# Output projection by pairs of token tiles, with the first feed-forward columns ahead of the last transposes

## The chip, the cores and the metric

The kernel runs on one core of one Trainium2 chip. The metric is the device time of one execution in microseconds (us). Before the change it is 950.52 us, the median of three runs (950.33 to 952.98). Engines are named as in the profile: PE (TensorE) does matmuls and transposes, PEld is its weight load, DVE (VectorE), ACT (ScalarE) and POOL (GpSimd) do elementwise work, and SP issues most DMAs.

## The reference, cut to what matters

One encoder block on 512 tokens and 16 learned meta tokens, width 1024, float32. Two branches (stick-breaking attention and gated linear attention) are merged by gates into `mix_in`; the change begins behind that.

```python
mix = (gate_sb * (sb @ w_sb_out) + gate_gla * (o @ w_gla_out)) @ w_o      # 528 x 1024
h = h + rmsnorm(mix, norm_mix_post)
hn = rmsnorm(h, norm_ffn_pre)
up = hn @ w_ffn_up                                                        # 528 x 2816
act = gelu(causal_dwconv(up, conv_w, conv_b))                             # 3 taps along the tokens
ffn = (act * (hn @ w_ffn_gate)) @ w_ffn_down
h = h + rmsnorm(ffn, norm_ffn_post)                                       # meta tokens dropped
```

## The kernel before, in words

Every float32 product is made of three fp32r matmuls: each operand is split into a high part (a cast on ACT) and a low part (operand minus high part), and high times high, high times low and low times high are added in PSUM. For a weight, `load_w` (lines 79 to 92) does one DMA from SP into a `raw` tile of 512 KB, one cast on ACT (`wh`, L90) and one subtraction on POOL (`wl`, L91). There are three `raw` buffers, and two `wh` and two `wl` buffers in the pool `wp`; a second pool `wx` has two more of each.

The output projection (`mix_in @ w_o`) works on four token tiles of 128 and on two column halves of 512. The right half of `w_o` (`woh`, `wol`) is loaded while the merged input is still being made (loop over `j` from L795). The left half comes in four loads `oa0` to `oa6`, each of two row blocks `k`; each load is used for all four token tiles (L909 to L919, 96 matmuls of 512 columns, "wo" in the trace), so all four left halves are finished together, in the two 1024-column PSUM buffers `wo01` and `wo23`. Those two are the only buffers of their tag (`mm`), which the feed-forward's `pt_up` uses later. The right half is done tile by tile in `second(i)` (24 matmuls each, "wob"), in PSUM buffers of tag `z` (two). The product for the two meta tokens that the convolution needs is made from the `raw` tiles by `meta_products` (L787), so a `raw` tile is held until those matmuls are done.

Behind each half `gained` (L835) takes the sum of squares on ACT and the gain on DVE; `normed` (L849) then does, for one token tile, two RMS norms, the residual and the product `y`, and transposes `y` on PE (8 transposes, "ht"), with a cast on ACT and a subtraction on DVE for each half (`split`, L136) into `h2h` and `h2l`, which hold the normed hidden state with the tokens along the columns. `mini` (L871) is the same chain for the two meta tokens, in pieces.

The feed-forward loops over 22 column tiles `m`: `pt_up` (L965, 48 matmuls of 256 or 258 columns, tokens 0 to 255 and then the others) and `ga` (L981 to L986). For `m` of 0 and 1 both are done in two token halves, so that tokens 0 to 255 (tiles 1 and 2) can be multiplied before tiles 3 and 4 are transposed.

The order on each engine is fixed before the run by a planner (`schedule_with_timeline_sim`, L1195). It goes by the program's order and lets later work pass ahead where it expects the earlier not to be ready; buffers are given out in the order in which they are taken. `tc.issue_after(x)` puts an instruction behind `x` in the queue of the same engine. Three such pins stand around the change: two transposes are set behind matmuls 8 and 16 of the last `second` (`CUT`, L928), and the casts of the first two gate tiles are set behind a step of tile 2's norm (`GA`, L944 and L979). Each engine takes its own queue strictly in that order.

Of the kernel before, what the change touches and what calls it, by code (L numbers as in the profile page):

```python
# [43 lines left out]
GA = 3  # L44
CUT = (8, 16)
# [6 lines left out]
def block_kernel(ctx: ExitStack, tc: tile.TileContext, x, meta_tokens, norm_mix_pre, w_in, w_gk_up, b_gk,  # L52
# [47 lines left out]
    def proj(w, xh, xl, segs, name, apart=False):  # L100

        wh, wl = w
        nk, m = wh.shape[1], wh.shape[2]
        (l0, l1), (_, l2) = segs
        pt = mmt(f"pt_{name}")
        segs = [(pt[:m, 512 - l1 + l0 : 512], l0, l1), (pt[:m, 512 : 512 + l2 - l1], l1, l2)]
        steps = [(k, a, b) for k in range(nk) for a, b in ((wh, xh), (wh, xl), (wl, xh))]
        for grp in ([[s] for s in segs] if apart else [segs]):
            for n, (k, a, b) in enumerate(steps):
                for dst, lo, hi in grp:  # L110
                    pe.matmul(dst, a[:, k, :], b[:, k, lo:hi], start=n == 0, stop=n == len(steps) - 1)  # L111
        return pt[:m, 512 - l1 + l0 : 512 + l2 - l1]
# [712 lines left out]
    with tc.tile_pool(name="pw", bufs=1) as pw:  # L825
# [22 lines left out]

        def normed(i):  # L849

            t, h, xi = slice((i - 1) * P, i * P), hb[:, i - 1, :], xr[:, i - 1, :]
# [7 lines left out]
            y = pw.tile([P, D], F32, tag="y", name=f"y{i}", bufs=2)  # L859
            for b in range(2):  # L860
                c = slice(b * 512, b * 512 + 512)
                dve.scalar_tensor_tensor(out=y[:, c], in0=h[:, c], scalar=r, in1=g2bc[:, c], op0=ALU.mult, op1=ALU.mult)
            for b in range(2):
# [38 lines left out]

        ones = pw.tile([P, P], F32, name="ones")
# [3 lines left out]
        pos = [mmt("wo01"), mmt("wo23")]  # L907
        d0 = [pos[i // 2][:, (i % 2) * 512 : (i % 2) * 512 + 512] for i in range(4)]
        for k in range(8):  # L909
            if k % 2 == 0:  # L910
                wh, wl = load_w(wrows(w_o, k, 2, 0, 512), 2, f"oa{k}")
                raw = last_raw[0]
            a, b = wh[:, k % 2, :], wl[:, k % 2, :]
            for i in range(4):
                t = slice(i * P + NM - T0, i * P + P + NM - T0)
                for q, (m, w) in enumerate(((mh, a), (mh, b), (ml, a))):
                    pe.matmul(d0[i], m[k][:, t], w, start=k == 0 and q == 0, stop=k == 7 and q == 2)  # L917
            if k % 2:
                meta_products(k - 1, 0, raw)  # L919

        last_mm = [None]

        def second(i):
# [3 lines left out]
            for q, (a, b) in enumerate(ops):  # L927
                after = sum(q >= c for c in CUT) if i == 4 else 0  # L928
                with tc.issue_after(last_ht[after].ins) if after else ExitStack():
                    last_mm[0] = pe.matmul(pt, a, b, start=q == 0, stop=q == len(ops) - 1)  # L930
# [32 lines left out]
    with tc.tile_pool(name="pu", bufs=2) as pu:  # L963
        for m in range(FT):
            pt = proj(load_w(cols(w_up, m * P), KT, f"up{m}", into=wx if m % 2 else None), h2h, h2l, FFNS, f"up{m}", apart=m < 2)  # L965
# [16 lines left out]
            for lo, hi in ((0, 256), (256, 512)) if m < 2 else ((0, 512),):  # L982
                for k in range(KT):
                    for q, (a, b) in enumerate(((wh, h2h), (wh, h2l), (wl, h2h))):
                        pe.matmul(pg_[:, lo:hi], a[:, k, :], b[:, k, lo:hi], start=lo == 0 and k == 0 and q == 0,  # L985
                                  stop=k == KT - 1 and q == 2, skip_group_check=True)  # L986
# [212 lines left out]
```

## Time and profile before

| what | value |
|---|---|
| median of three runs | 950.52 us |
| profiled execution | 952.2 us |
| its span in the trace | 950.5 us |
| PE busy | 924.2 us, 97% of the span |
| DVE, ACT, POOL busy | 67%, 52%, 37% |
| granted PE clock, mean | 0.992 of full |

The profiled execution is 1.7 us above the median and 1.7 us longer than its own span. A row of a timeline gives the start in us from the span's beginning, the time of the group, and in square brackets how long the engine stood idle before it and what released it. The end of a matmul is modelled and overlaps the next one, so the pace is read from start to start. The granted clock is a share of 2.4 GHz; 0.5 is 1.2 GHz.

### The profile page before, as it was taken

The page shows a single profiled execution, that of the slowest core. Times are in us where ns is not written, and L with a number is a line of the kernel's source. Part 1 is how long each engine was busy: PE and PEld are TensorE (multiplying, and loading weights), DVE is VectorE, ACT ScalarE, POOL GpSimd, SP SyncE. Part 2 cuts the span into 40 slices and gives each one's busy share as a digit, 9 for nine tenths or more (in the row PEclk, how much of TensorE's full clock was granted, in tenths as well). Part 3 has the DMA queues.
Part 4 walks back from the last instruction along what each step waited for, and adds up shares of the span by engine and source line. Part 5 has one row for each costly group of instructions (what it writes and reads, how often), then busy time and mean ns, then how long its engine had stood idle before and what let it go on. Part 6 is the DMA issues. An engine that isn't in the chain of part 4 may idle for free.

```text
span 950.5 us, 17905 instructions
## 1 busy us (share of the span) xinstructions
PE 924.2 (97%) x7229; PEld 846.2 (89%) x7229; DVE 632.4 (67%) x1080; ACT 492.2 (52%) x934; POOL 351.3 (37%) x259
## 2 busy tenths in 40 slices
PE   7999999999999998999999998999999999999996
PEld 7999999999999998999998677999999999988785
DVE  6676858677558785887847347555554445588987
ACT  5664656566467674676664244533333333355654
POOL 5433242333345444554445432444444444100100
PEclk9999999999999999999999998999999999999999
DMA  7122222212222212231214643333333333274923
GB/s 212 53 69 68 69 68 68 68 46 72 65 75 80 67 48 66 67 90 46 78 56 130 212 124 112 89 104 98 89 89 90 100 99 89 89 258 159 266 81 123
DMA packets 129876, 93.39 MB, mean 98 GB/s; under 512 B 4080, under 2 KB 114930, under 8 KB 129794
## 3 DMA queue, kind: packets, MB, share of 16 engines
q1 hardware_dynamic: 126178, 82.55, 29.1%
q10 hardware_dynamic: 2112, 6.82, 1.9%
q0 software_dynamic: 1504, 2.88, 1.8%
q8 instruction: 57, 0.93, 0.4%
q14 instruction: 25, 0.20, 0.1%
HBM read 88.05 MB, written 4.19 MB: 97 GB/s over the span
## 4 chain that ended last, share of the span: by engine, by line
PE 86%; DVE 7%; issue 2%; ACT 2%; POOL 1%; SPq 1%; DMA 1%; DVEq 0%; POOLq 0%; ACTq 0%
PE pt_up L111 13%; PE ga L985 13%; PE pt_gv L111 5%; PE pt_gr L111 5%; PE pt_mg L111 4%; PE pt_go L111 4%; PE pt_ms L111 3%; PE dA L1047 3%; PE dD L1047 3%; PE pt_gk L111 3%; PE pt_so L111 2%; PE pt_gq L111 2%; PE dB L1047 2%; PE wo L917 2%; PE pt_sv L111 2%
## 5 line engine op out<-in xcount | busy, mean ns | idle before, releaser
L91 POOL TENSOR_TENSOR wl_up<-raw_up,wh_up 128x1024 fp32r<-128x1024 f32 x22 | 52.9, 2407 | 85.1 <-ACT wh_up L90 85.1
L91 POOL TENSOR_TENSOR wl_ga<-raw_ga,wh_ga 128x1024 fp32r<-128x1024 f32 x22 | 55.6, 2530 | 71.9 <-ACT wh_ga L90 71.9
L111 PE MATMUL pt_up<-h2l,wh_up 128*128 128x256 f32 (+1 forms) x352 | 73.5, 283 | 0.0
L111 PE MATMUL pt_up<-h2h,wh_up 128*128 128x256 f32 (+1 forms) x352 | 73.4, 283 | 0.0
L111 PE MATMUL pt_up<-h2h,wl_up 128*128 128x256 f32 (+1 forms) x352 | 73.4, 282 | 0.0
L985 PE MATMUL ga<-h2l,wh_ga 128*128 128x512 f32 (+1 forms) x192 | 72.2, 376 | 0.2 <-DVE h2l L139 0.2
L985 PE MATMUL ga<-h2h,wh_ga 128*128 128x512 f32 (+1 forms) x192 | 72.0, 376 | 0.2 <-ACT h2h L138 0.2
L985 PE MATMUL ga<-h2h,wl_ga 128*128 128x512 f32 (+1 forms) x192 | 72.1, 376 | 0.0
L90 ACT CAST wh_up<-raw_up 128x1024 fp32r<-128x1024 f32 x22 | 23.1, 1050 | 79.2 <-PE pt_up L111 67.2
L111 PEld LDWEIGHTS pt_up<-h2h,wh_up 128*128 128x128 f32 x352 | 57.0, 189 | 1.8
L111 PEld LDWEIGHTS pt_up<-h2l,wh_up 128*128 128x128 f32 x352 | 55.5, 189 | 0.0
L111 PEld LDWEIGHTS pt_up<-h2h,wl_up 128*128 128x128 f32 x352 | 55.4, 189 | 0.0
L985 PEld LDWEIGHTS ga<-h2h,wl_ga 128*128 128x128 f32 x192 | 36.2, 188 | 7.0
L985 PEld LDWEIGHTS ga<-h2l,wh_ga 128*128 128x128 f32 x192 | 36.1, 188 | 6.6 <-DVE h2l L139 0.4
L985 PEld LDWEIGHTS ga<-h2h,wh_ga 128*128 128x128 f32 x192 | 36.1, 188 | 6.6 <-ACT h2h L138 0.5
L976 DVE SCALAR_TENSOR_TENSOR cy<-pt_up,cw,cy 128x511 f32<-128x511 f32 (+1 forms) x22 | 16.4, 746 | 36.8 <-ACT cy L973 36.8
L976 DVE SCALAR_TENSOR_TENSOR yp<-pt_up,cw,yp 128x511 f32<-128x511 f32 (+1 forms) x22 | 16.4, 745 | 31.2 <-ACT yp L973 31.2
L90 ACT CAST wh_ga<-raw_ga 128x1024 fp32r<-128x1024 f32 x22 | 22.9, 1047 | 26.1 <-PE ga L985 24.3
L138 ACT CAST sh_p<-As 128x512 fp32r<-128x512 f32 (+1 forms) x30 | 17.4, 584 | 29.6 <-PE dB L1047 12.9
L91 POOL TENSOR_TENSOR wl_gr<-raw_gr,wh_gr 128x1024 fp32r<-128x1024 f32 x8 | 19.1, 2387 | 36.0 <-ACT wh_gr L90 27.1
L1075 POOL DMA_DIRECT2D tv<-in_w_ffn_down_dram x6 | 7.1, 1177 | 68.2 <-DVE wl_p L139 68.2
L111 PE MATMUL pt_gr<-hnh,wh_gr 128*128 128x258 f32 (+1 forms) x128 | 28.2, 294 | 0.0
(558 smaller groups left out, 3179.4 us busy)
## 6 DMA issues: line engine op xcount, KB each, us to landing
raw_up<-in_w_ffn_up_dram SPq DMA_DIRECT2D x22, 512.0 KB, 3.8
raw_ga<-in_w_ffn_gate_dram SPq DMA_DIRECT2D x22, 512.0 KB, 3.8
raw_t<-in_w_ffn_down_dram SPq DMA_DIRECT2D x10, 512.0 KB, 7.2
raw_gv<-in_w_in_dram SPq DMA_DIRECT2D x8, 512.0 KB, 3.9
raw_gr<-in_w_in_dram SPq DMA_DIRECT2D x8, 512.0 KB, 3.8
raw_mg<-in_w_in_dram SPq DMA_DIRECT2D x8, 512.0 KB, 3.9
raw_go<-in_w_gla_out_dram SPq DMA_DIRECT2D x8, 512.0 KB, 4.2
raw_ms<-in_w_in_dram SPq DMA_DIRECT2D x8, 512.0 KB, 3.9
```

Source lines behind the costliest of these rows:

```text
L90: act.copy(hi_out, raw)
L91: lo_eng.tensor_tensor(out=lo_out, in0=raw, in1=f32(hi_out), op=ALU.subtract)
L111: pe.matmul(dst, a[:, k, :], b[:, k, lo:hi], start=n == 0, stop=n == len(steps) - 1)
L138: act.copy(hi, src)
L917: pe.matmul(d0[i], m[k][:, t], w, start=k == 0 and q == 0, stop=k == 7 and q == 2)
L976: dve.scalar_tensor_tensor(out=y[:, d:], in0=pt[:, : SEQ - d], scalar=c, in1=y[:, d:], op0=ALU.mult, op1=ALU.add)
L985: pe.matmul(pg_[:, lo:hi], a[:, k, :], b[:, k, lo:hi], start=lo == 0 and k == 0 and q == 0, stop=k == KT - 1 and q == 2, skip_group_check= ...
L1047: mm[i] = pe.matmul(dsts[i], a, b, start=first and k == 0 and j == 0, stop=last and k == NP - 1 and j == 2, skip_group_check=True)
L1075: return lambda n, q, nk: pool.dma_start(out=t[:, q : q + nk, :], in_=block(s, c, q, nk), accum_op=ALU.add)
```

## The change

The left half of the projection is done by `halves(g)` for two token tiles at a time: first tiles 1 and 2 into `wo12`, later tiles 3 and 4 into `wo34`. Each of the two passes loads all four row-block pairs, so the left half of `w_o` is fetched, cast and subtracted twice. The right halves of tiles 1 and 2 go ahead of the first pass. The norm chain of tiles 1 and 2 (`mixed`, which is `gained` twice and `normed`) stands between the passes, and behind it the weights of the first two `up` tiles, both into `wx`. The transposes are taken out of `normed` into `turned`; those of tiles 1 and 2 are pinned behind the second pass. Then come `second(3)`, `second(4)` with the pieces of `mini`, the weights of the first two gate tiles, and for tokens 0 to 255 the products of the first two `up` and the first two gate tiles; the transposes of tile 3 are pinned behind the first of these gate products, those of tile 4 behind the second. The loop over `m` then does only the rest of these four products. The pins `CUT` and `GA` are gone.

```diff
-        pos = [mmt("wo01"), mmt("wo23")]
-        d0 = [pos[i // 2][:, (i % 2) * 512 : (i % 2) * 512 + 512] for i in range(4)]
-        for k in range(8):
-            if k % 2 == 0:
-                wh, wl = load_w(wrows(w_o, k, 2, 0, 512), 2, f"oa{k}")
-                raw = last_raw[0]
-            a, b = wh[:, k % 2, :], wl[:, k % 2, :]
-            for i in range(4):
...
+        pos = [mmt("wo12"), mmt("wo34")]
+        def halves(g):
+            for k in range(8):
+                if k % 2 == 0:
+                    wh, wl = load_w(wrows(w_o, k, 2, 0, 512), 2, f"oa{g}{k}")
+                    raw = last_raw[0]
+                a, b = wh[:, k % 2, :], wl[:, k % 2, :]
+                for i in range(2):
+                    t = slice((2 * g + i) * P + NM - T0, (2 * g + i + 1) * P + NM - T0)
+                    for q, (m, w) in enumerate(((mh, a), (mh, b), (ml, a))):
+                        last_mm[0] = pe.matmul(pos[g][:, i * 512 : i * 512 + 512], m[k][:, t], w, start=k == 0 and q == 0, stop=k == 7 and q == 2)
+                if k % 2 and g == 0:
+                    meta_products(k - 1, 0, raw)
+
+        def mixed(i, pt):
+            gained(i, pos[(i - 1) // 2][:, (i - 1) % 2 * 512 : (i - 1) % 2 * 512 + 512], 0)
+            gained(i, pt, 1)
+            normed(i)
...
-        gained(1, second(1), 1)
-        for i in (1, 2, 3, 4):
-            gained(i, d0[i - 1], 0)
+        early = [second(1), second(2)]
+        halves(0)
+        for i in (1, 2):
+            mixed(i, early[i - 1])
+        ups = [load_w(cols(w_up, m * P), KT, f"up{m}", into=wx) for m in range(2)]
+        halves(1)
+        with tc.issue_after(last_mm[0].ins):
+            turned(1)
+            turned(2)
         m = mini()
-        for i in (2, 3, 4):
+        for i in (3, 4):
             pt = second(i)
-            if i > 2:
-                with tc.issue_after(last_mm[0].ins):
-                    next(m)
-            gained(i, pt, 1)
-            normed(i - 1)
-            if i == GA:
-                late = last_exp[0]
+            with tc.issue_after(last_mm[0].ins):
+                next(m)
+            mixed(i, pt)
+        gas = [load_w(cols(w_gate, m * P), KT, f"ga{m}") for m in range(2)]
         next(m)
-        normed(4)
+
+        begun = [proj(ups[m], h2h, h2l, FFNS, f"up{m}", apart=True, only=(0,)) for m in range(2)]
+        pgs_ = []
+        for m in range(2):
+            pgs_.append(pst(f"ga{m}", "z"))
+            gate_half(pgs_[m], gas[m], 0, 256)
+            with tc.issue_after(last_ga[0].ins):
+                turned(3 + m)
...
-            pt = proj(load_w(cols(w_up, m * P), KT, f"up{m}", into=wx if m % 2 else None), h2h, h2l, FFNS, f"up{m}", apart=m < 2)
+            if m < 2:
+                pt = proj(ups[m], h2h, h2l, FFNS, f"up{m}", apart=True, only=(1,), pt=begun[m])
+            else:
+                pt = proj(load_w(cols(w_up, m * P), KT, f"up{m}", into=wx if m % 2 else None), h2h, h2l, FFNS, f"up{m}")
...
-            with tc.issue_after(late.ins) if m < 2 else ExitStack():
-                wh, wl = load_w(cols(w_gate, m * P), KT, f"ga{m}", into=wx if m % 2 else None)
-            pg_ = pst(f"ga{m}", "z")
...
+            if m < 2:
+                pg_ = pgs_[m]
+                gate_half(pg_, gas[m], 256, 512)
+            else:
+                pg_ = pst(f"ga{m}", "z")
+                gate_half(pg_, load_w(cols(w_gate, m * P), KT, f"ga{m}", into=wx if m % 2 else None), 0, 512)
```

## Rows read from the trace of the kernel before

**Rows 1.** the page: busy shares, and the chain that ended last by engine.

```profile
PE 924.2 (97%) x7229; PEld 846.2 (89%) x7229; DVE 632.4 (67%) x1080; ACT 492.2 (52%) x934; POOL 351.3 (37%) x259
...
PE 86%; DVE 7%; issue 2%; ACT 2%; POOL 1%; SPq 1%; DMA 1%; DVEq 0%; POOLq 0%; ACTq 0%
```

**Rows 2.** busy time of PE, PEld, DVE, ACT, POOL; clock; DMA share; GB/s.

```profile
526.00:544.00 18.00, 18.00 (x93) 12.46 (x91) 6.12 (x6) 2.56 (x4) 4.26 (x3) 1.00 0.66 235
...
572.00:582.00 10.00, 6.28 (x25) 5.22 (x26) 7.50 (x17) 4.70 (x12) 5.27 (x2) 0.66 0.49 156
```

**Rows 3.** PE in order of time: start, us, line, operation, tiles.

```profile
566.62 0.40 PE L930 MATMUL wob<-wol,mh 128*128 128x512 f32 x1
567.81 1.38 PE L867 MATMUL ht<-ident,y 128*128 128x128 f32 x8 [0.79 <-DVE y L862]
568.94 0.48 PE L930 MATMUL wob<-woh,ml 128*128 128x512 f32 x1
...
570.64 0.40 PE L930 MATMUL wob<-woh,mh 128*128 128x512 f32 x1
570.97 0.71 PE L880 MATMUL mini<-sel,mc 128*32 128x2 f32 x64
574.04 1.09 PE L867 MATMUL ht<-ident,y 128*128 128x128 f32 x4 [2.36 <-DVE y L862]
...
577.55 0.78 PE L930 MATMUL wob<-wol,mh 128*128 128x512 f32 x1
...
580.96 0.28 PE L111 MATMUL pt_up<-h2h,wh_up 128*128 128x256 f32 x1
```

**Rows 4.** the same view, at full pace, and around the last tile's transposes.

```profile
559.32 0.39 PE L930 MATMUL wob<-woh,mh 128*128 128x512 f32 x1
...
564.68 0.40 PE L930 MATMUL wob<-woh,ml 128*128 128x512 f32 x1
...
584.37 0.28 PE L985 MATMUL ga<-h2h,wl_ga 128*128 128x256 f32 x1
...
586.87 0.28 PE L985 MATMUL ga<-h2h,wl_ga 128*128 128x256 f32 x1
...
589.03 0.60 PE L867 MATMUL ht<-ident,y 128*128 128x128 f32 x4
589.39 0.37 PE L111 MATMUL pt_up<-h2h,wh_up 128*128 128x256 f32 x1
...
593.67 1.07 PE L867 MATMUL ht<-ident,y 128*128 128x128 f32 x8
...
595.71 0.39 PE L985 MATMUL ga<-h2l,wh_ga 128*128 128x256 f32 x1 [0.23 <-DVE h2l L139]
```

**Rows 5.** the same view, where the first four row blocks of L917 end.

```profile
543.39 0.40 PE L917 MATMUL wo<-wh_oa,ml 128*128 128x512 f32 x1
...
544.26 0.50 PE L930 MATMUL wob<-woh,mh 128*128 128x512 f32 x1
```

**Rows 6.** DMA queue of SP, in order of time.

```profile
519.40 19.08 SPq L85 DMA_DIRECT2D raw_oa<-in_w_o_dram  x4
...
549.10 0.37 SPq L85 DMA_DIRECT2D raw_up<-in_w_ffn_up_dram  x1
```

**Rows 7.** ACT in order of time, the third cast of L917's weights.

```profile
543.18 1.05 ACT L90 CAST wh_oa<-raw_oa 128x1024 fp32r<-128x1024 f32 x1 [11.32 <-DMA raw_oa<-in_w_o_dram]
```

**Rows 8.** POOL in order of time: subtractions of L917's weights and of the gate's.

```profile
544.31 4.76 POOL L91 TENSOR_TENSOR wl_oa<-raw_oa,wh_oa 128x1024 fp32r<-128x1024 f32 x2 [12.84 <-ACT wh_oa L90]
...
573.62 5.27 POOL L91 TENSOR_TENSOR wl_ga<-raw_ga,wh_ga 128x1024 fp32r<-128x1024 f32 x2 [14.77 <-ACT wh_ga L90]
```

**Rows 9.** the page: DMA issues, KB each, median us to landing.

```profile
raw_up<-in_w_ffn_up_dram SPq DMA_DIRECT2D x22, 512.0 KB, 3.8
```

**Rows 10.** one tile, y: duration ns min/median/max, first and last start.

```profile
L862 DVE SCALAR_TENSOR_TENSOR y<-hb,a_ffn,g2bc x8: 744/748/2846, 567.0 to 593.2; 128x512 f32<-128x512 f32 x8
```

**Rows 11.** DVE in order of time, the last tile's y.

```profile
592.49 1.42 DVE L862 SCALAR_TENSOR_TENSOR y<-hb,a_ffn,g2bc 128x512 f32<-128x512 f32 x2
```

More of the change, by code (lines that the diff above doesn't have):

```diff
@@ L43 @@
 EASY = 4
-GA = 3
-CUT = (8, 16)
 EARLY = 3
@@ L98, in wrows, with proj @@
         return w[k0 * P : (k0 + nk) * P, c0:c1].rearrange("(k p) m -> p k m", p=P)
-    def proj(w, xh, xl, segs, name, apart=False):
+    last_pr = [None]
+    def proj(w, xh, xl, segs, name, apart=False, only=None, pt=None):
         wh, wl = w
@@ L104, in proj @@
         (l0, l1), (_, l2) = segs
-        pt = mmt(f"pt_{name}")
+        begins = only and pt is None
+        pt = mmt(f"pt_{name}") if pt is None else pt
         segs = [(pt[:m, 512 - l1 + l0 : 512], l0, l1), (pt[:m, 512 : 512 + l2 - l1], l1, l2)]
         steps = [(k, a, b) for k in range(nk) for a, b in ((wh, xh), (wh, xl), (wl, xh))]
+        segs = [segs[i] for i in only] if only else segs
         for grp in ([[s] for s in segs] if apart else [segs]):
@@ L110, in proj @@
                 for dst, lo, hi in grp:
-                    pe.matmul(dst, a[:, k, :], b[:, k, lo:hi], start=n == 0, stop=n == len(steps) - 1)
-        return pt[:m, 512 - l1 + l0 : 512 + l2 - l1]
+                    last_pr[0] = pe.matmul(dst, a[:, k, :], b[:, k, lo:hi], start=n == 0, stop=n == len(steps) - 1)
+        return pt if begins else pt[:m, 512 - l1 + l0 : 512 + l2 - l1]
     last_exp = [None]
@@ L901, in mini, with gate_half @@
             yield
+        last_ga = [None]
+        def gate_half(pt, w, lo, hi):
+            wh, wl = w
+            for k in range(KT):
+                for q, (a, b) in enumerate(((wh, h2h), (wh, h2l), (wl, h2h))):
+                    last_ga[0] = pe.matmul(pt[:, lo:hi], a[:, k, :], b[:, k, lo:hi], start=lo == 0 and k == 0 and q == 0,
+                                           stop=k == KT - 1 and q == 2, skip_group_check=True)
         ones = pw.tile([P, P], F32, name="ones")
         pool.memset(ones, 1.0)
-        pos = [mmt("wo01"), mmt("wo23")]
-        d0 = [pos[i // 2][:, (i % 2) * 512 : (i % 2) * 512 + 512] for i in range(4)]
-        for k in range(8):
-            if k % 2 == 0:
-                wh, wl = load_w(wrows(w_o, k, 2, 0, 512), 2, f"oa{k}")
-                raw = last_raw[0]
-            a, b = wh[:, k % 2, :], wl[:, k % 2, :]
-            for i in range(4):
[L915 to L919, printed above, removed]
-        last_mm = [None]
+        pos = [mmt("wo12"), mmt("wo34")]
+        last_mm = [None]
+        def halves(g):
[14 more added lines that the diff above has]
+            normed(i)
         def second(i):
@@ L927, in second @@
             for q, (a, b) in enumerate(ops):
-                after = sum(q >= c for c in CUT) if i == 4 else 0
-                with tc.issue_after(last_ht[after].ins) if after else ExitStack():
-                    last_mm[0] = pe.matmul(pt, a, b, start=q == 0, stop=q == len(ops) - 1)
-            return pt
-        gained(1, second(1), 1)
-        for i in (1, 2, 3, 4):
-            gained(i, d0[i - 1], 0)
+                last_mm[0] = pe.matmul(pt, a, b, start=q == 0, stop=q == len(ops) - 1)
+            return pt
+        early = [second(1), second(2)]
[7 more added lines that the diff above has]
+            turned(2)
         m = mini()
-        for i in (2, 3, 4):
+        for i in (3, 4):
             pt = second(i)
-            if i > 2:
-                with tc.issue_after(last_mm[0].ins):
-                    next(m)
-            gained(i, pt, 1)
-            normed(i - 1)
-            if i == GA:
-                late = last_exp[0]
-        next(m)
-        normed(4)
+            with tc.issue_after(last_mm[0].ins):
+                next(m)
+            mixed(i, pt)
+        gas = [load_w(cols(w_gate, m * P), KT, f"ga{m}") for m in range(2)]
+        next(m)
+        begun = [proj(ups[m], h2h, h2l, FFNS, f"up{m}", apart=True, only=(0,)) for m in range(2)]
[5 more added lines that the diff above has]
+                turned(3 + m)
         for i in range(4):
```

12 lines of the change are left out of this document (5 added, 7 removed).

## The prediction, made before the changed kernel had run

> **What bounds the kernel now.** Three views are read, from the coarse to the fine. The page comes first: PE is busy for 97% of the span and makes 86% of the chain that ended last [rows 1]. With the same matmuls before and after, time can only come from stretches in which PE stands still or runs slowly, so the next view is the busy time by stretch. In 526 to 544, where the left half of the projection runs, PE is busy for all 18.00 us at a clock of 1.00. In 572 to 582 it is busy for 6.28 of 10.00 us, and the mean clock is 0.66, so part of what is left runs at 1.2 GHz [rows 2]. The third view, PE in order of time, says what the holes are [rows 3]. I count them from start to start against the full pace: 23 steps of 512 columns take 564.68 - 559.32 = 5.36 us, 0.233 each; 21 steps of 256 columns take 2.50 us, 0.119 each; four transposes between matmuls take 0.36 us, so eight take 0.72 [rows 4].
>
> The holes [rows 3]:
> - From the end of the matmul at 566.62 (566.62 + 0.23 = 566.85) to the next projection matmul at 568.94 are 2.09 us with 0.72 us of transposes in them: 1.37 lost, waiting for `y` of tile 1.
> - From 570.64 + 0.23 = 570.87 to 577.55 are 6.68 us with 0.71 of `mini` and 0.72 of transposes: 5.25 lost, waiting for `y` of tile 2.
> - From 577.55 to 580.96 are 3.41 us for eight matmuls of 0.233 (1.86): 1.55 lost. PE had just stood idle, and the clock stands at its lower level.
>
> Together 8.2 us: the most that this change can take out here. The wait behind the last tile's transposes (2.04 us from 593.67 to 595.71, of which 0.72 are transposes, so 1.3 [rows 4]) stays, since tile 4 is still the last.
>
> **What the change leaves equal.** L917 has 8 x 4 x 3 = 96 matmuls before and 2 x 8 x 2 x 3 = 96 after. The 96 of `second`, the transposes, and the products of the first two `up` and gate tiles (already in two halves of the tokens before) are the same in number and shape. PE's own work changes by nothing.
>
> **What goes.** The norms of tiles 1 and 2 can start when the first pass ends, with 48 matmuls of the second pass (48 x 0.233 = 11.2 us) ahead of their transposes. Tile 3's transposes have three half products, 3 x 24 x 0.119 = 8.6 us, ahead of them and tile 4's have four, 11.4 us; before, they were set between the last eight projection matmuls and the first feed-forward ones. If the norms are done in time, all three holes go: -8.2 us.
>
> **What the second fetch costs.** Four more loads are issued on SP. Before, each load fed 24 matmuls, 24 x 0.233 = 5.6 us; now each feeds 12, 2.8 us. For each, ACT casts for 1.05 us [rows 7] and POOL subtracts for 2.4 (4.76 for two [rows 8]), 3.5 us one behind the other; with two buffers for the split weights, the third load waits until PE has done with the first. So loads are now slower than PE wherever PE has nothing else. SP's queue matters as well: it waited in the midst of its four issues of these loads, which stretch over 19.08 us, for the three raw buffers, and the buffer of the fourth came free for a later weight at 549.10, when POOL ended [rows 6, 8]. In the new order the first `up` weights stand ahead of the second pass on SP, ACT and POOL. Nothing else queued on these engines there is on the path; what waits behind are the second pass's own weights.
>
> POOL's queue from 544.31 [rows 8] is then eight subtractions: two for the first pass, two for `up`, four for the second pass. 8 x 2.4 = 19.2 brings it to 563.5. A raw buffer freed at 549.10 and a landing of 3.8 [rows 9] and a cast of 1.05 give 554.0, about when POOL comes to it (544.31 + 4 x 2.4 = 553.9), so the transfers hide behind POOL. The third load of the pass waits for PE to free a buffer: its predecessor's twelve matmuls, a cast and the hand-over cost POOL some 1.9. So the last subtraction ends near 565.4, and eleven matmuls behind it end the second pass near 568.0.
>
> PE meanwhile: the 48 matmuls of row blocks 0 to 3 end at 543.6 before, and ten matmuls of `second` still come behind them from 544.26 on [rows 5]. Now only 24 are there, and the ten come first: 543.6 - 24 x 0.233 + 10 x 0.233 = 540.3. The next weights are cast at 543.18 whatever PE does, since their transfer sets it [rows 7]. From 540.3 to 568.0 are 27.7 us; PE has 72 matmuls of L917 (16.8) and the meta products (1.1) for it. A hole of 9.8 us is left, and what can fill it are the 48 matmuls of tiles 3 and 4's right half, 11.2 us. They need the PSUM buffers of tiles 1 and 2, which come free after a square and a gain; ACT stands idle for 11.32 us just there [rows 7]. The planner does such filling today: ten `second` matmuls stand where the third load comes late [rows 5]. The bounds are 0 (filled) and 9.8 (not). I take it as filled, but with POOL late: DVE operations with two operands in SBUF and POOL's subtractions hold each other up. One `y` took 2846 ns against a median of 748 [rows 10], during two subtractions that took 5.27 together where two took 4.76 [rows 8]. Some five of the norms' eight such operations fall on POOL's chain and push it by 5 x 0.6 = 3.0: the pass ends at 571.0, PE's own work at 540.3 + 17.9 + 11.2 = 569.4, and 1.6 us are lost.
>
> The Trainium skill, "SBUF — State Buffer", section "Who interferes with whom", says that a DVE instruction with two inputs in SBUF and a GpSimd instruction that reads SBUF exclude each other for a whole instruction. The long `y` agrees. By that rule alone each of the eight operations can wait a whole subtraction, which is the slower rival below and not my sum.
>
> **What is late next.** With the filler used up, nothing covers the split of tiles 1 and 2 behind their transposes. The bounds are 0 (some `second` left over) and 2.6 (twice the wait of one tile [rows 4]); I take that one wait, 1.3. Then tile 4: before, 592.49 + 1.42 - 580.96 = 12.9 us lay between the end of its projection [rows 3] and its `y` [rows 11]. In the new order tile 3's norm starts at the same moment and four splits and the gate's subtractions lie beside. The cover is 1.4 (transposes) + 1.3 + 0.7 (`mini`) + 11.4 + 0.4 = 15.2. Four more DVE splits at some 0.7, an estimate from the 1.3 above, make 15.7, so 0.5 is lost; the bounds are 0 and 4.2, where two `y` meet the gate's subtractions (2.1 each [rows 10]). The pins that kept these subtractions away are gone.
>
> **Sum.** -8.2 + 1.6 + 1.3 + 0.5 = -4.8 us. The profiled execution took 952.2, which gives 947.4; it lies 1.7 above the median of the runs shown, so against 950.5 the forecast is 945.7. By the bounds of the last terms it lies between 943.0 and 948.0.
>
> **Rivals.**
> - Everything hides: 950.5 - 8.2 = 942.3. For it speaks that the filler (11.2) is larger than the hole (9.8); against it, that POOL has no slack.
> - The gain is given back in the two passes, because the filler is only partly put into the holes: some half of 9.8 stays, 4.9 in place of 1.6, with the split and tile 4's lateness as above: -8.2 + 4.9 + 1.8 = -1.5, 949.0; its range is 947.7 to 953.3. For it speaks that PE takes its queue in order, so a filler set behind a late weight helps nothing; against it, that the planner's filling before fits the transfers [rows 5].
> - Slower: the transposes of tiles 1 and 2 wait for `y` at the head of PE's queue. They are pinned behind the second pass, and DVE must do eight two-operand operations beside POOL's closed chain of eight subtractions. At 2.85 us each [rows 10] they take 22.8 us; from some 554.5, when the first squares and gains are done, `y` of tile 2 comes at 577.3 where my sum has PE ready at 571.0. That is 6.3 lost, and with the idle time the lower clock as in the third hole, 1.5. With 1.6, 1.3 and 2.6 for tile 4, which starts later on DVE, the sum is -8.2 + 13.3 = +5.1: 955.6. It decides from the point where more than about six of the eight wait out a subtraction. For it speaks the one long `y`; against it, that POOL's chain ends near 568, after which nothing holds DVE.
>
> **How the numbers follow.** Chances: forecast 0.42, everything hides 0.15, given back 0.25, slower 0.18. About 0.3%, 2.9 us, is what a measurement of this kernel can tell from no change. Faster by more than that (below 947.6): the first two, 0.57. Within it (947.6 to 953.4): nearly all of the third and a little of the others, 0.25. Slower: 0.18. The range that leaves out 2 in 10 is 941.9 to 953.3: it takes in everything hidden and the third case, and leaves out the slower one. The forecast's own range is 943.0 to 948.0.
>
> **What would show it.** The three holes gone: PE without idle time ahead of the transposes of tiles 1 and 2, and at clock 1.00 up to the feed-forward. Matmuls of tiles 3 and 4's right half among those of L917. POOL closed with eight subtractions and PE's second pass ending near 568 to 571. The prediction is wrong if L917 stands still for more than 2 us in its passes, if the first transposes wait for `y` for more than 2 us, or if the hole comes back at tile 4's transposes.

## The result, and the profile after

The changed kernel takes 957.56 us (median of six runs, 955.25 to 959.0) against 951.55 for the kernel before on the same chip: a ratio of 1.006, interval 1.0042 to 1.0078. It is slower by 0.6%; the forecast was 945.7, and the range ended at 953.3.

The page shows no change that would explain it: PE's busy time is 1.4 us longer than in [rows 1], and its share of the span and of the chain are the same. The page of after, busy shares and the chain by engine:

```profile
PE 925.6 (97%) x7229; PEld 847.4 (89%) x7229; DVE 640.5 (67%) x1080; ACT 496.6 (52%) x938; POOL 360.7 (38%) x263
...
PE 86%; DVE 6%; issue 2%; ACT 2%; DMA 2%; POOL 1%; DVEq 0%; ACTq 0%; POOLq 0%; SPq 0%
```

So the place must be found by stretch. From the first right-half matmul to the first matmul of the third `up` tile, the same work lies in both kernels: 103.6 us before (503.44 to 607.03), 111.1 after (502.06 to 613.12), 7.5 more. The profiled execution of after took 957.73, 5.5 more than before's: its earlier part was 1.4 shorter, the part behind 0.6. The stretches of [rows 2] in after, with those behind each of them (columns as there):

```profile
526.00:544.00 18.00, 14.91 (x81) 9.06 (x79) 4.86 (x6) 2.61 (x3) 4.14 (x4) 1.00 0.72 257
544.00:560.00 16.00, 13.26 (x48) 9.68 (x49) 6.00 (x8) 8.22 (x14) 12.95 (x6) 0.79 0.58 175
...
572.00:582.00 10.00, 8.20 (x41) 6.33 (x39) 6.05 (x8) 4.45 (x10) 6.84 (x3) 1.00 0.40 122
582.00:596.00 14.00, 13.03 (x145) 12.79 (x146) 12.02 (x38) 7.50 (x26) 0.30 (x1) 0.76 0.33 115
```

526 to 544, where PE was full before, now has 3.1 us without work, and the clock falls in the stretch behind. 572 to 582 is better than before (8.20 in place of 6.28, clock 1.00), and 582 to 596 has the low clock that used to stand there. PE in after, in order of time:

```profile
539.18 0.61 PE L793 MATMUL meta<-raw_oa,m 128*2 128x256 f32 x8
541.68 0.61 PE L793 MATMUL meta<-raw_oa,m 128*2 128x256 f32 x8 [1.89 <-DMA raw_oa<-in_w_o_dram]
542.83 0.50 PE L936 MATMUL wo<-wh_oa,mh 128*128 128x512 f32 x1 [0.54 <-ACT wh_oa L88]
544.21 0.70 PE L793 MATMUL meta<-raw_oa,m 128*2 128x256 f32 x8 [0.88 <-DMA raw_oa<-in_w_o_dram]
545.26 0.79 PE L936 MATMUL wo<-wl_oa,mh 128*128 128x512 f32 x1 [0.34 <-POOL wl_oa L89]
545.85 0.63 PE L936 MATMUL wo<-wh_oa,ml 128*128 128x512 f32 x1
...
548.25 0.40 PE L936 MATMUL wo<-wh_oa,ml 128*128 128x512 f32 x1
...
552.77 0.50 PE L936 MATMUL wo<-wh_oa,mh 128*128 128x512 f32 x1 [0.65 <-ACT wh_oa L88]
554.81 0.79 PE L950 MATMUL wob<-woh,mh 128*128 128x512 f32 x1 [1.53 <-DVE hb L842]
...
578.04 1.04 PE L875 MATMUL ht<-ident,y 128*128 128x128 f32 x8
...
581.13 0.66 PE L875 MATMUL ht<-ident,y 128*128 128x128 f32 x4 [1.59 <-DVE h2l L141]
582.97 1.12 PE L875 MATMUL ht<-ident,y 128*128 128x128 f32 x4 [1.18 <-DVE v_mix L125]
...
588.99 0.29 PE L917 MATMUL ga<-h2h,wl_ga 128*128 128x256 f32 x1
```

Counted from start to start against the pace of [rows 4], as before, and a group of eight meta products at the 0.55 us that it takes where nothing waits:
- In the first pass, from 539.18 to 545.26, 4.2 us are lost waiting for the left half's weights; behind that the matmuls run at half pace until 548.25 (seven steps: one of 0.59, five of 0.43, a last one of 0.27), 1.4 lost. At 552.77 and 554.81 another 2.6 are lost, and 1.7 of low clock up to 558.33. Together 9.9: 6.8 of waiting and 3.1 of low clock.
- The second pass runs at full pace and ends at 578.04. The transposes of tile 1 follow at once. Those of tile 2 lose 3.2 us of waiting at 581.13 and 582.97, and until 588.99 PE runs at half pace: 2.7. Together 5.9.
- The three holes of [rows 3], 8.2, are gone. The last transposes lose 1.6 where the same count gives 1.1 before.

-8.2 + 9.9 + 5.9 + 0.5 = 8.1 against the 7.5 measured in the stretch; 0.6 is not assigned.

Why does nothing fill the first hole? ACT and DVE in after, around the end of the first pass:

```profile
541.74 1.04 ACT L88 CAST wh_oa<-raw_oa 128x1024 fp32r<-128x1024 f32 x1 [11.13 <-DMA raw_oa<-in_w_o_dram]
...
552.63 0.59 ACT L841 ACTIVATE wj<-wo 128x512 f32<-128x512 f32 x1
...
553.34 0.60 ACT L841 ACTIVATE wj<-wob 128x512 f32<-128x512 f32 x1
```

```profile
553.34 0.69 DVE L842 TENSOR_TENSOR hb<-wo,g1bc 128x512 f32<-128x512 f32 x1 [22.01 <-DMA raw_oa<-in_w_o_dram]
554.06 0.69 DVE L842 TENSOR_TENSOR hb<-wob,g1bc 128x512 f32<-128x512 f32 x1
```

ACT stands idle for 11.13 us, as it did before [rows 7], but the right half's square (`wj<-wob`) does not use them: it comes at 553.34, behind the left half's (`wj<-wo`) at 552.63, and its gain at 554.06. The matmul at 554.81, the first of tile 3's right half, is released by that gain: until then both buffers of tag `z` hold the right halves of tiles 1 and 2. The squares of both halves write into one scratch buffer (`junk`). `mixed` takes it for the left half first, and buffers are given out in the order in which the program takes them.

### The profile page after: what moved, and what is told of

Read it like the earlier page. It is cut to its first block, busy times and chain, and to the rows that moved or that the text cites. A ratio compares the mean times of both kernels' runs of the same rounds, so it can differ in the third digit from the quotient of the medians.

```text
span 956.0 us, 17918 instructions
## 1 busy us (share of the span) xinstructions
PE 925.6 (97%) x7229; PEld 847.4 (89%) x7229; DVE 640.5 (67%) x1080; ACT 496.6 (52%) x938; POOL 360.7 (38%) x263
## 4 chain that ended last, share of the span: by engine, by line
PE 86%; DVE 6%; issue 2%; ACT 2%; DMA 2%; POOL 1%; DVEq 0%; ACTq 0%; POOLq 0%; SPq 0%
PE pt_up L113 13%; PE ga L917 13%; PE pt_gv L113 5%; PE pt_gr L113 4%; PE pt_mg L113 4%; PE pt_ms L113 4%; PE pt_go L113 4%; PE dA L1078 3%; PE dD L1078 3%; PE wob L950 3%; PE pt_gk L113 3%; PE pt_so L113 2%; PE pt_gq L113 2%; PE dB L1078 2%; PE pt_sv L113 2%
## 5 line engine op out<-in xcount | busy, mean ns | idle before, releaser
L917 PE MATMUL ga<-h2l,wh_ga 128*128 128x512 f32 (+1 forms) x192 | 72.3, 377 | 0.0
L917 PE MATMUL ga<-h2h,wh_ga 128*128 128x512 f32 (+1 forms) x192 | 72.3, 377 | 0.0
L917 PE MATMUL ga<-h2h,wl_ga 128*128 128x512 f32 (+1 forms) x192 | 72.2, 377 | 0.0
L917 PEld LDWEIGHTS ga<-h2h,wl_ga 128*128 128x128 f32 x192 | 36.4, 190 | 7.0
L917 PEld LDWEIGHTS ga<-h2l,wh_ga 128*128 128x128 f32 x192 | 36.4, 190 | 6.2
L917 PEld LDWEIGHTS ga<-h2h,wh_ga 128*128 128x128 f32 x192 | 36.4, 190 | 6.0
L89 POOL TENSOR_TENSOR wl_oa<-raw_oa,wh_oa 128x1024 fp32r<-128x1024 f32 x8 | 19.3, 2415 | 24.8 <-ACT wh_oa L88 24.6
```

What stands on the lines that cost most here:

```text
L89: lo_eng.tensor_tensor(out=lo_out, in0=raw, in1=f32(hi_out), op=ALU.subtract)
L917: last_ga[0] = pe.matmul(pt[:, lo:hi], a[:, k, :], b[:, k, lo:hi], start=lo == 0 and k == 0 and q == 0, stop=k == KT - 1 and q == 2, skip_ ...
```

## The experiments

Each kernel was timed against the kernel before on the same chip. "Stretch" is the time from the first right-half matmul to the third `up` tile, as above, in its profiled execution (103.6 before, 111.1 after).

| kernel | median | before | ratio, interval | stretch |
|---|---|---|---|---|
| e2_columns_only | 952.2 | 950.63 | 1.0012, 1.0002 to 1.0021 | 103.8 |
| e3_pairs_only | 967.53 | 950.63 | 1.0172, 1.0157 to 1.0187 | 119.3 |
| e1_release | 953.81 | 950.63 | 1.0032, 1.0018 to 1.0047 | 106.7 |
| e4_keep | 956.12 | 950.63 | 1.0057, 1.0038 to 1.0075 | 107.6 |
| f_after | 954.5 | 951.67 | 1.0028, 1.0016 to 1.0041 | 106.7 |
| f_before | 951.71 | 951.67 | 0.9999, 0.9989 to 1.0009 | 103.4 |
| e6_release_pin | 952.57 | 951.67 | 1.0006, 0.9996 to 1.0016 | 104.2 |
| f_e7 | 951.84 | 951.67 | 1.0003, 0.9993 to 1.0013 | 103.2 |
| f_e9 | 952.27 | 951.8 | 1.0008, 0.9999 to 1.0017 | 104.8 |
| f_e10 | 956.72 | 951.8 | 1.0057, 1.0043 to 1.0072 | 108.6 |
| f_e11 | 951.79 | 950.7 | 1.0004, 0.9995 to 1.0013 | 103.1 |
| f_e12 | 952.69 | 950.7 | 1.001, 1.0001 to 1.0019 | 104.2 |

### Each part alone

The expectations speak of three theories. A: the buffers that the filling matmuls need are not free in time. B: the second fetch is too slow. C: the order of the transposes is the fault. A and B are taken up in the next part.

The second part alone: one pass over four tiles as before, the first two `up` and gate tiles ahead. In the code of all runs "..." stands for lines left out.

```diff
-        def halves(g):
+        def halves():
...
-                for i in range(2):
...
+                for i in range(4):
...
-        early = [second(1), second(2)]
-        halves(0)
-        for i in (1, 2):
-            mixed(i, early[i - 1])
...
-        halves(1)
...
+        halves()
+        for i in (1, 2):
+            gained(i, second(i), 1)
+        for i in (1, 2):
+            gained(i, pos[0][:, (i - 1) * 512 : i * 512], 0)
+            normed(i)
```

> The second part of the change alone: the left half is done in one pass for four tiles with one fetch, as before; the transposes of tiles 1 and 2 are pinned behind the right half of tile 4, and the first columns of two up and two gate tiles stand ahead of the transposes of tiles 3 and 4, as in the change. Theories A and B both put the loss into the two passes, so this part keeps most of the 8.2 us of the holes, less some 3 to 4 for the split of tiles 1 and 2 that nothing covers: 946 to 948. Theory C (the order of the transposes is the fault: in the changed kernel 3.6 us of waiting and 2.4 us of low clock around the transposes of tile 2): 951 to 955.

The first part alone: two passes, and the `up` and gate loads and products back in the loop over `m`.

```diff
-        ups = [load_w(cols(w_up, m * P), KT, f"up{m}", into=wx) for m in range(2)]
...
+            turned(i)
...
-        begun = [proj(ups[m], h2h, h2l, FFNS, f"up{m}", apart=True, only=(0,)) for m in range(2)]
...
-            gate_half(pgs_[m], gas[m], 0, 256)
...
+            pt = proj(load_w(cols(w_up, m * P), KT, f"up{m}", into=wx if m % 2 else None), h2h, h2l, FFNS, f"up{m}", apart=m < 2)
```

> The first part alone: two passes with the second fetch and the transposes of tiles 1 and 2 behind the second pass, as in the change; the first up and gate tiles and their loads stand in the loop again and the transposes of tiles 3 and 4 directly behind their norms. Theories A and B: the holes in the passes stay as in the changed kernel, 956 to 960. Theory C: the loss goes with the moved columns, 950 to 953.

The second part alone makes 1.0012, 0.2 us more in the stretch: with the norms where they were it gains nothing. Its 952.2 lies in theory C's range and not in that of A and B. The wait of [rows 3] for tile 2's `y` is still there. PE of e2_columns_only:

```profile
572.63 0.40 PE L896 MATMUL msmix<-msqmix,ones 128*128 128x16 f32 x2 [1.99 <-DVE h2l L141]
575.24 1.89 PE L875 MATMUL ht<-ident,y 128*128 128x128 f32 x8 [2.21 <-DVE y L866]
```

The first part alone costs 15.7 us of stretch, more than any theory allowed for, and the 950 to 953 that theory C gave for it is out. It has the first hole of after in its passes (of the second only 0.63 us is left), and behind them two longer ones: one ahead of tile 2's transposes, and one for the split of the last tiles, which the products of the columns cover in after. PE of e3_pairs_only:

```profile
584.31 1.97 PE L875 MATMUL ht<-ident,y 128*128 128x128 f32 x8 [6.38 <-DVE h2l L141]
...
614.57 0.70 PE L113 MATMUL pt_up<-h2h,wh_up 128*128 128x258 f32 x2 [4.91 <-ACT h2h L140]
```

So the loss sits in the first part, and the two parts don't add: 15.7 + 0.2 alone, 7.5 together.

### What empties the passes

Two theories: the right halves' buffers are not free because their squares wait for the scratch buffer's turn, or the loads of the second fetch are too slow for PE whatever stands beside them. The first is tested twice: by the program's order, and by the place that the square writes to.

```diff
+        for i in (1, 2):                            # e1_release
+            gained(i, early[i - 1], 1)
         halves(0)
         for i in (1, 2):
-            mixed(i, early[i - 1])
+            gained(i, pos[0][:, (i - 1) * 512 : i * 512], 0)
+            normed(i)
```

> The changed kernel with one edit: square and gain of the right halves of tiles 1 and 2 stand ahead of the first pass, so that their two PSUM buffers come free before it. Theory A (release): the trace of the changed kernel has PE waiting 4.2 us at 539.7 to 545.3 and 2.6 us at 552.0 to 554.8, with 3.0 us of low clock behind them, because the matmuls that should fill these holes could not get a buffer before the gain at 554.06; with the edit they fill them, 9.8 us go, some 2 come back where POOL's subtractions end later than the filler lasts: 949 to 951. Theory B (second fetch): the second pass ends when POOL's and ACT's queue of loads ends, whatever PE does in between: 956 to 958.

```diff
-            junk = pw.tile([P, 512], F32, tag="junk", name=f"wj{i}_{hf}")       # f_after, f_before
-            act.activation(junk, pt, AF.Square, accum_out=sq[:, i, hf : hf + 1])
+            act.activation(hb[:, i - 1, c], pt, AF.Square, accum_out=sq[:, i, hf : hf + 1])
```

> The changed kernel with its order as it is and one edit: the squares of the two halves are written over the slice of hb that the gain then fills, in place of the one scratch buffer (junk) that all squares share. Theory A, made sharper: the right halves of tiles 1 and 2 kept their PSUM buffers because the one scratch buffer is given out in program order, left half first; with the edit the holes of 9.8 us in the passes close without any reordering, as in the run with the moved gains, and tile 2's squares no longer stand behind tile 1's norm: 950 to 953. Rival (the gain's place in the program decides, not the scratch buffer): 956 to 958.

> The kernel before with only the scratch buffer taken out of the four halves' squares. Theory A and D: there the right halves' buffers are not what PE waits for, and the order of PE hardly changes, but tile 2's squares can go ahead of tile 1's norm, so the waits for y (6.6 us) shrink by up to 2: 948.5 to 950.5. Rival: no change, 950 to 951.

The second theory is tested by fetching less: the second pass begins with the row blocks 4 to 7 that are still held.

```diff
-            for k in range(8):                                                  # e4_keep
+            ks = (4, 5, 6, 7, 0, 1, 2, 3) if g else range(8)
+            for k in ks:
                 if k % 2 == 0:
-                    wh, wl = load_w(wrows(w_o, k, 2, 0, 512), 2, f"oa{g}{k}")
+                    if not (g and k >= 4):
+                        held[k] = load_w(wrows(w_o, k, 2, 0, 512), 2, f"oa{g}{k}")
+                    wh, wl = held[k]
```

> The changed kernel with two loads fewer: the second pass begins with row blocks 4 to 7, whose split weights are still in their buffers, and fetches only row blocks 0 to 3 again. Theory B (second fetch): two casts (2.1 us), two subtractions (4.8 us) and two transfers of 512 KB go, and the second pass starts without waiting for a load: 951 to 953. Theory A (release): the wait of 4.2 us for the third load of the first pass and the low clock behind it (1.4) stay, the 2.6 us between the passes and the 1.7 behind them go: 953 to 954.

Either way of freeing the squares fills the passes, though both times (953.81 and 954.5) lie above what theory A gave for them. The stretches 526 to 544 and 544 to 560 in f_after, where only the place of the squares is changed:

```profile
526.00:544.00 18.00, 18.00 (x90) 12.13 (x89) 6.04 (x8) 3.60 (x7) 4.21 (x4) 1.00 0.74 255
544.00:560.00 16.00, 16.00 (x81) 11.90 (x80) 5.79 (x9) 8.44 (x15) 13.31 (x6) 1.00 0.62 175
```

3.09 and 2.74 us of idle time and the low clock are gone, with the four extra loads still there. What is left in the passes is one wait for a late subtraction. PE of e1_release and then of f_after:

```profile
565.21 0.50 PE L936 MATMUL wo<-wl_oa,mh 128*128 128x512 f32 x1 [1.26 <-POOL wl_oa L89]
```

```profile
565.72 0.51 PE L935 MATMUL wo<-wl_oa,mh 128*128 128x512 f32 x1 [1.86 <-POOL wl_oa L89]
```

Lost there are 1.4 and 2.0. With two loads fewer and the scratch buffer as it was (e4_keep) 3.8 us stay, all in the first hole, released by the DMA as in after; the second hole is gone, and so is the low clock (1.00 in both stretches), though PE had stood idle for nearly as long as in after. Its time is above both ranges all the same; now tile 2's transposes wait for `y`, and the mean clock of 572 to 582 is 0.68:

```profile
541.40 0.61 PE L793 MATMUL meta<-raw_oa,m 128*2 128x256 f32 x8 [1.72 <-DMA raw_oa<-in_w_o_dram]
...
578.25 1.94 PE L875 MATMUL ht<-ident,y 128*128 128x128 f32 x8 [4.64 <-DVE y L866]
```

So both have a part, of different kinds. That the loads are slower than PE makes the holes, and with fewer loads the loss shrinks from 9.9 to 3.8. What stays is the first hole, 4.2 before: it lies in the first pass, whose four loads are the same, and PE has only two tiles' matmuls for them where it had four. That nothing fills the holes is the scratch buffer's doing, and with it out of the way all four extra loads cost 1.4 to 2.0. In the kernel before the same edit does nothing (0.9999): there, no right half waits on a later left half.

But only 4.3 of these 9.9 us come back in the stretch, by either edit. As soon as the passes are full, the second pass ends some 7 us sooner, and tile 2's transposes wait. PE of f_after:

```profile
571.20 1.03 PE L874 MATMUL ht<-ident,y 128*128 128x128 f32 x8
578.95 1.97 PE L874 MATMUL ht<-ident,y 128*128 128x128 f32 x8 [6.72 <-DVE h2l L141]
```

### What makes tile 2 late

In e1_release the second transposes wait 4.91 us for tile 1's split, which DVE does behind tile 2's `y`; and `y` takes 3.50 where it takes 1.42 in after, while POOL does two gate subtractions (572.35, 5.25 for both). DVE of e1_release:

```profile
571.87 3.50 DVE L866 SCALAR_TENSOR_TENSOR y<-hb,a_ffn,g2bc 128x512 f32<-128x512 f32 x2
```

The casts of these gate tiles were kept behind the last cast of tile 2's transposes, first alone and then with all of the above and two loads fewer.

```diff
-        gas = [load_w(cols(w_gate, m * P), KT, f"ga{m}") for m in range(2)]
+        with tc.issue_after(last_split[0].ins):     # e6_release_pin: e1_release with this
+            gas = [load_w(cols(w_gate, m * P), KT, f"ga{m}") for m in range(2)]
```

> The run with the gains moved ahead of the first pass (953.8), and the casts of the two gate tiles pinned on ACT behind the last cast of tile 2's transposes. Theory D (what is left is the lateness of tile 2's transposes: in that run y of tile 2 took 3.50 us for 1.42 beside the gate's first subtraction, and the casts of tile 1's transposes stood behind 2.06 us of gate casts): 2 to 4 us go, 950 to 952. If the wait is set by DVE's own work alone: 953 to 954.5.

f_e7 is e1_release, f_after, e4_keep and this pin in one.

> Everything together: the gains ahead, no shared scratch buffer for them, the gate's casts pinned, and the second pass beginning with row blocks 4 to 7 from their buffers, so that only two loads are fetched twice. Theory D: four of the DVE operations that wait out a subtraction do so no more and y of tile 2 comes 4 to 6 us earlier than at 575.4: 945 to 949. If DVE's chain for two norms is itself the bound: 949 to 952.

The pin gives back 2.5 us of e1_release's stretch; `y` of tile 2 takes 1.41 again. f_e7 has no loss in its passes, but not the time that was expected from it; one wait is left, with matmuls at half pace behind it until 583.28. PE of f_e7, and DVE of f_e7 in tile 1's norm:

```profile
575.19 1.32 PE L876 MATMUL ht<-ident,y 128*128 128x128 f32 x8 [3.82 <-DVE v_mix L125]
```

```profile
558.41 2.05 DVE L134 SCALAR_TENSOR_TENSOR a_mix<-a_mix,r_mix 128x1 f32<-128x1 f32 x1
560.50 3.65 DVE L860 SCALAR_TENSOR_TENSOR hb<-hb,a_mix,xr 128x512 f32<-128x512 f32 x2
```

Two subtractions of POOL lie there (558.05, 4.89 for both). The next two kernels start from f_e7 and are meant to take POOL away from the norms; the `up` and the gate tiles change their pools.

```diff
-                        held[k] = load_w(wrows(w_o, k, 2, 0, 512), 2, f"oa{g}{k}")
+                        held[k] = load_w(wrows(w_o, k, 2, 0, 512), 2, f"oa{g}{k}", into=wx if g else None)   # not in f_e10
...
-        ups = [load_w(cols(w_up, m * P), KT, f"up{m}", into=wx) for m in range(2)]
         halves(1)
+        with tc.issue_after(late.ins):              # late: tile 2's last Exp
+            ups = [load_w(cols(w_up, m * P), KT, f"up{m}") for m in range(2)]
...
-            gas = [load_w(cols(w_gate, m * P), KT, f"ga{m}") for m in range(2)]
+            gas = [load_w(cols(w_gate, m * P), KT, f"ga{m}", into=wx) for m in range(2)]
```

> As the kernel f_e7, and POOL is kept off the norms: the two loads that are fetched again are cast into the other pool of split weights, so that they need no buffer of the first pass and POOL can be done with them sooner, and the first two up weights are loaded behind the second pass, their casts pinned behind tile 2's last norm step. Theory D (what is left behind the second pass in f_e7, 4.1 us of waiting and some 2.6 of low clock, is the norm chain of tile 2, lengthened by DVE operations that wait out POOL's subtractions): no DVE operation of the two norms is over 2 us, y of tile 2 comes some 4 us sooner than the 572.5 of f_e7, and the wait ahead of tile 2's transposes is under 1: 944 to 947. Rival E (the chain of the two norms is as long without POOL): y of tile 2 within 1.5 us of f_e7's, 951 to 952. Rival F (the wait moves to the up weights, whose subtractions now come late): transposes without a wait, but the first up product waits over 2 us for wl_up: 949 to 952.

> As f_e9, but the two loads that are fetched again stay in the pool of the first pass, so that only the up weights are taken from the norms. Theory D: POOL's two subtractions of these loads still meet the norms; one or two DVE operations stay over 2 us, y of tile 2 some 2 us sooner than in f_e7: 947 to 950. Rival E: as f_e7, 951 to 952. Rival F: 949 to 953, with the wait at the first up product.

Both miss. In f_e9 tile 1's norm is free of POOL, but the pin let both `up` subtractions start just ahead of tile 2's `y`. POOL of f_e9, then DVE:

```profile
570.46 5.12 POOL L89 TENSOR_TENSOR wl_up<-raw_up,wh_up 128x1024 fp32r<-128x1024 f32 x2 [16.20 <-ACT wh_up L88]
```

```profile
570.48 5.65 DVE L867 SCALAR_TENSOR_TENSOR y<-hb,a_ffn,g2bc 128x512 f32<-128x512 f32 x2
```

In f_e10 the two left-half subtractions meet tile 1's norm again (L134 2.05, L860 3.65), `y` of tile 2 takes 3.51, and the wait grows to 7.47. In the last two kernels DVE does the `up` subtractions itself, behind tile 2's `y`; in f_e12 only the first of them, and POOL does the second, whose cast is pinned behind the last cast of tile 2's transposes.

```diff
+        late, done = last_exp[0], last_y[0]
         halves(1)
+        with tc.issue_after(late.ins), tc.issue_after(done.ins):
-            ups = [load_w(cols(w_up, m * P), KT, f"up{m}") for m in range(2)]
+            ups = [load_w(cols(w_up, m * P), KT, f"up{m}", lo_eng=dve) for m in range(2)]
```

> As f_e9, whose norms met POOL only once, at y of tile 2: its casts' pin let both up subtractions begin at 570.46 and y at 570.48, 5.65 for the two halves. Here both up subtractions are done by DVE, pinned behind y of tile 2, so POOL is idle from the last oa subtraction to the gate's. Theory D (what is left is DVE waiting out POOL): y of tile 2 is done by 572, each half under 0.8; the wait ahead of tile 2's transposes is under 0.7, the low clock behind it is gone; a wait for h2l or wl_up of up to 1.5 us can stay, since DVE now has two more subtractions of some 1.4: 945 to 949. Rival E (the two norms take as long without POOL): y of tile 2 after 574, 951 to 952. Rival F (DVE's two subtractions hold up the splits as long as POOL held up y): y by 572, but over 2.5 us of waiting between the transposes and the up products: 950 to 953.

> As f_e11, but only the first up tile is subtracted by DVE; the second's casts are pinned behind the last cast of tile 2's transposes, and POOL subtracts it. Theory D: as f_e11, with 1.4 less of DVE's work ahead of the splits: 944 to 949, not slower than f_e11 by more than 1. Rival F: the second up tile's wl comes late, over 1 us of waiting inside the up products: 949 to 952. Rival E: 951 to 952.

DVE of f_e11, and then its PE behind the passes:

```profile
569.07 1.41 DVE L868 SCALAR_TENSOR_TENSOR y<-hb,a_ffn,g2bc 128x512 f32<-128x512 f32 x2
570.40 2.35 DVE L89 TENSOR_TENSOR wl_up<-raw_up,wh_up 128x1024 fp32r<-128x1024 f32 x2
```

```profile
570.15 0.60 PE L877 MATMUL ht<-ident,y 128*128 128x128 f32 x4
571.81 0.50 PE L113 MATMUL pt_up<-h2h,wh_up 128*128 128x256 f32 x2 [1.06 <-ACT h2h L143]
573.41 0.66 PE L877 MATMUL ht<-ident,y 128*128 128x128 f32 x4 [1.11 <-DVE h2l L144]
574.79 0.78 PE L890 MATMUL mini<-sel,mc 128*32 128x2 f32 x64 [0.72 <-DVE h2l L144]
...
588.71 0.39 PE L898 MATMUL msffn<-msqffn,ones 128*128 128x16 f32 x2 [1.45 <-ACT msqffn L895]
...
593.09 0.39 PE L113 MATMUL pt_up<-h2h,wh_up 128*128 128x258 f32 x1 [0.83 <-ACT h2h L143]
```

The part of theory D about tile 2 holds: with POOL away, `y` takes 1.41 and is done at 570.5, 68.5 us behind the first right-half matmul at 502.02, where f_e7 has 70.6 (573.86 less 503.26); and tile 2's first transposes stand at 570.15 with no wait. Its time does not hold: 951.79, and the stretch is 103.1 as in f_e7. In place of one wait of 3.82 there are now three for the splits (2.89 of idle time), one of 1.45 for the meta tokens, whose matmul stands at the head of PE's queue, and 0.83 for the last split. Nor is the low clock gone: the mean of 572 to 582 is 0.83, and 14 matmuls from 575.50 to 578.66 lose 1.5. That is what rival F expected in time and place, with more to it than the two subtractions on DVE, which took 2.35.

f_e12, with one subtraction less on DVE, waits less at the first splits (1.87 in three waits) and has a clock of 1.00 in 572 to 582. But it waits more at the last ones, where the first row of three is this (PE of f_e12):

```profile
591.30 0.65 PE L877 MATMUL ht<-ident,y 128*128 128x128 f32 x4 [0.62 <-DVE mssffn L900]
```

With 0.88 at 592.83 and 0.68 at 594.17 that makes 2.18 where f_e11 has 0.83, and matmuls at half pace follow it. The stretch is 104.2, 1.1 above f_e11's, and no matmul waits for the second `up` tile's late subtraction, which rival F had named. No kernel of this study beats the one before.

## Why the prediction was wrong

- **PE's work equal**: right. The number of matmuls is the same (7229 in both pages).
- **The three holes go, -8.2**: right as a count. The waits for `y` of [rows 3] are gone; what is lost at the same transposes now is counted below, as the split.
- **"I take it as filled"**: this is the step that failed. The bounds were 0 and 9.8; 9.9 was measured. That the two agree so closely is luck: 9.8 was waiting alone, and of the 9.9 6.8 are waiting and 3.1 low clock, which the sum had left out. The reason given, that the `z` buffers "come free after a square and a gain; ACT stands idle for 11.32 us just there", looked at the engine and not at the operands of the square: it writes `junk`, a single buffer, and the left half of the same tile had been given it first. The planner's filling in the kernel before, on which the choice rested [rows 5], showed only that matmuls can pass, with buffers that were free. The given-back rival named a half of it, for another reason.
- **POOL late, 1.6**: not to be seen in after, because the holes gave POOL time. In the kernels whose passes are filled the last subtractions are late by 1.4 (e1_release), 2.0 (f_after) and 1.9 (e6_release_pin). The size fits, but not by the way it was worked out: POOL's chain was to be closed and pushed by 0.6 for each of five operations, a price that no row gives. POOL had stood idle for 4.5 to 4.8 us ahead of the last two subtractions, waiting for the cast, and these two took 5.3 to 5.6 in place of 4.76.
- **The split of tiles 1 and 2, 1.3, bounds 0 and 2.6**: mis-sized: 3.2 of waiting and 2.7 of low clock, over its upper bound. The 1.3 was itself read 0.2 too large, since two gate matmuls lie in it; the same count gives 1.1. ACT had more to do just there than the row for one tile shows. ACT in after:

```profile
578.24 0.60 ACT L841 ACTIVATE wj<-wo 128x512 f32<-128x512 f32 x1 [1.90 <-PE wo L936]
...
578.83 1.04 ACT L88 CAST wh_ga<-raw_ga 128x1024 fp32r<-128x1024 f32 x1
579.76 0.59 ACT L140 CAST h2h<-ht 128x512 fp32r<-128x512 f32 x1
```

  The first cast of tile 1's transposes (`h2h<-ht`) stands behind tile 3's square and a gate cast. The pins that kept gate casts away were counted for POOL's sake and for tile 4 only; taking them out costs here. How much is not known by itself: the 2.5 us of e6_release_pin hold it together with the 2.1 by which `y` got shorter, and no run parts the two. And a stall of PE was priced without the half-speed matmuls that can follow it, though the third hole of [rows 3] was just such a row.
- **Tile 4, 0.5**: 1.6 lost against 1.1, as said.
- **The slower rival** had the right sign and the wrong place in after: `y` of tile 2 was done at 575.9, ahead of the end of the second pass at 578.04, so its transposes waited for tile 1's splits and not for `y`. Its mechanism came up as soon as the first hole was mended: 3.50 and 5.65 us for a `y` that takes 1.41 without POOL. With the passes as forecast it does count: in f_after, which is the forecast's case, the second pass ends at 571.20, `y` of tile 2 at 575.89 and the first of tile 1's splits, which DVE does behind it, just ahead of 578.95, where the transposes go on; the ratio is 1.0028.
- **The range**: "by the bounds of the last terms" does not give 943.0 to 948.0. With 0 to 2.6 for the split and 0 to 4.2 for tile 4 it would have been 943.9 to 950.7.
- **The sum**: with filled passes and POOL away (f_e11) the stretch is 0.5 us shorter, not 4.8. The matmuls that fill the passes are those that before stood between the splits. The last sentence on that, "with the filler used up, nothing covers the split", was right and took one wait of one tile for what is two tiles and the meta tokens.

That the scratch buffer kept the passes from being filled is shown twice, by two edits that leave all loads in place. That POOL lengthens the norms is shown by the rows of f_e9 and f_e11. That the splits, the meta tokens and the low clock behind them are what is left at the end is read from f_e11's trace; no run covered them.

## What to carry to other kernels

Before a hole is counted as filled, follow the buffer that the filler needs back to what frees it, with every operand of the freeing operation, scratch outputs too: a single scratch buffer that is given out in program order ties together two chains that share nothing else. And when the same amount of work is moved from one gap to another, ask what covered the gap it leaves: here 8.2 us went and came back, first in the passes, then at `y`, then at the splits.

## What the runs showed of the hardware

- A stall of about the same length is not always followed by the low clock. In after the first hole (4.2 us lost by 545.26) is followed by half pace, five steps of 0.43 among them; in e4_keep, with 3.8 lost in the same place, the clock of the next stretch is 1.00. What decides between them no run here tells apart. Windows of e4_keep:

```profile
526.00:544.00 18.00, 15.04 (x84) 9.08 (x86) 4.59 (x6) 2.33 (x3) 4.03 (x4) 1.00 0.75 258
544.00:560.00 16.00, 15.60 (x72) 12.23 (x73) 4.35 (x7) 8.53 (x13) 12.90 (x7) 1.00 0.56 171
```

- DVE operations of one element per partition wait out POOL's subtractions too. In after, the last step of the norm's factor (L134, 128x1, two operands in SBUF) took 2.05 us beside a subtraction, and 0.16 without:

```profile
563.52 0.16 DVE L134 SCALAR_TENSOR_TENSOR a_ffn<-a_ffn,r_ffn 128x1 f32<-128x1 f32 x1
...
565.74 3.62 DVE L859 SCALAR_TENSOR_TENSOR hb<-hb,a_mix,xr 128x512 f32<-128x512 f32 x2
...
572.39 2.05 DVE L134 SCALAR_TENSOR_TENSOR a_ffn<-a_ffn,r_ffn 128x1 f32<-128x1 f32 x1
```

  POOL subtracts from 565.74 for 2.41 and from 572.03 for 2.40. The gain and the split, which read PSUM and one operand in SBUF, keep 0.69 and 0.68 beside them. The Trainium skill, "SBUF — State Buffer", section "Who interferes with whom", states the exclusion by operands in SBUF, and the rows agree; what the prediction left out is that a tiny operation pays as much as a large one, so that operations must be counted and not bytes.
- DVE takes the two subtractions of 128x1024 in 2.35 us (f_e11), POOL in 4.8 [rows 8]. Where DVE is the engine that would wait POOL out, doing the work itself can be the shorter way for the operation that would have waited: `y` of tile 2 is done 4 us earlier in f_e11 than in f_e9 (68.5 us behind the first right-half matmul in place of 72.5). The kernel as a whole hardly gained by it (1.0004 and 1.0008).
